# Two-layer hybrid encoder: order of the head products, value products and first weight splits

## The chip, the cores and the metric

The kernel runs on one core of one Trainium2 chip. The metric is the device time of one execution in microseconds (us), lower is better. Before the change it is 1668.3 us, the median of 3 runs (1664.87 to 1670.17). TensorE is called PE here, VectorE DVE, ScalarE ACT, GpSimd POOL and SyncE SP, as in the profile.

## The reference, cut to what matters

512 tokens, model width 1024, 8 heads, everything in float32.

```python
hn  = rms_norm(h, norm_mix[0]);  h += mlstm_mixer(hn, ...)               # layer 0
h  += swiglu(rms_norm(h, norm_ffn[0]), w_gate[0], w_up[0], w_down[0])
h  += sigmoid(rms_norm(h, norm_ple[0]) @ ple_gate[0]) * (p[0] @ ple_proj[0])
hn  = rms_norm(h, norm_mix[1])                                            # layer 1
proj = (hn @ b_w_in).reshape(B, S, 3, 3, 8, 128)       # group g, (q, k, v), head
# per group: rope(q), rope(k); window attention with dilation 1, 4, 16; merge by denominators
h  += o @ b_w_out[0]
h  += swiglu(rms_norm(h, norm_ffn[1]), ...);  h += (gated input);  out = rms_norm(h)
```

`rms_norm` is a factor per token, 1/sqrt(mean square + eps), times a weight per column. The factor per token can be multiplied in after a product, so a product with `hn` needs only the residual `h` times the column weight; the factor is needed when the product leaves PSUM.

## The kernel before, in words

**Residual and operands.** The residual is held transposed, as 8 tiles `hT[k]` of 128 columns x 512 tokens. `Norm.add(k)` (line 175) takes a finished `hT[k]`, multiplies by the column weights and splits the result into a rounded part `xh[k]` and a rest `xl[k]`, so that each product of two matrices is three matmuls (`mm3`, line 123: lines 124, 125, 126). `Norm.square(k)` adds the squares up in `q`; `Norm.stats` (line 244) makes the factor per token (`rcol`) with 8 small matmuls and five POOL operations; `Norm.bcast` (line 251) spreads it over all partitions as `rB`, either through two DMAs (lines 261 and 263) or, with `by_pe`, through 8 matmuls (line 255) and one DVE copy (line 258).

**Weights.** A weight tile of up to 1 MB comes by a DMA on SP's queue into one of 4 buffers (`wst`); `wsplit` (lines 116 and 117) splits it into `wh` on ACT and `wl` on DVE, 3 buffers each.

**PSUM.** There are 8 banks: 3 under the name `pj`, 3 under `s`, 2 under `o`. SBUF tiles of 2 KB per partition (`u`) share 58 buffers.

**Order.** The program is unrolled. Each engine's instructions are put in order when the program is built: earlier in the text goes first among those that the builder reckons to be ready at that moment. On the chip every engine then follows its fixed order.

**Layer 0's end and layer 1's start.** `ple(0)` (line 628) makes the 8 gate products and finishes `hT[0..7]` one by one: lines 658 (times `rB`), 659 (sigmoid), 660, 661 (add to `hT`), then `n1.add(k)`. `n1` also keeps sums of quarter blocks (`quad_sums`, lines 214 to 222, split in lines 207 and 208).

**Values.** `value_cell(g)` (line 773), three times, makes the values of group g for all heads with 7 instead of 8 block products (`product`, lines 784 to 797). Its weights are four quarters of 1 MB, added or subtracted in place on DVE (lines 807, 810). Its results are scaled by `rcol` (lines 803, 839) and stored to DRAM (lines 804, 840). In the first cell, between the fourth and the fifth product, come `n.stats()` and `n.bcast()` (lines 828, 829). After the third cell the tables `RS` and `RC` are multiplied by `rB` (lines 850 to 853).

**Heads.** `qk_head(h)` (line 887) makes q and k of three groups, 6 products of 24 matmuls, each evicted by `rope_evict` (line 855: DVE lines 858 and 860, POOL lines 861 and 863). `scores` (line 930) makes the probabilities, with two exchanges through DRAM (`swap`, line 739). `attend` (line 981) multiplies by the values. Before, the order is: three value cells, q and k of head 0, scores of head 0; then for each head h: values from DRAM (every second head), q and k of head h+1, `attend(h)`, scores of head h+1.

**Last head.** For the last head there are no next q and k; the loop computes the first 7 of 8 terms of three column blocks of `b_w_out` (`out_part`, line 1023) and finishes them after `attend`; the fourth block follows whole, then `colproj` (line 551) makes blocks 4 to 7. `residual` (line 566) adds each block to `hT` (line 568) and calls `nf.add`.

**Feed-forward.** `ffn` (line 580) begins with the first 256 columns of `w_gate` and `w_up`. It comes after `nf.stats()` and `nf.bcast()` in the text.

Of the kernel before, what the change touches and what calls it, by code (L numbers as in the profile page):

```python
# [15 lines left out]
ALU = mybir.AluOpType  # L16
# [20 lines left out]
def encoder_kernel(  # L37
# [513 lines left out]
    def colproj(src, xh, xl, nk, evict, ncols, first=0):  # L551

        for c2 in range(first, ncols // 256):
            o = [ps(), ps()]
            for k0 in range(0, nk, KT):
                kn = min(KT, nk - k0)
                st = wload(src, k0 * P, kn, 256 * c2)
                for cc in range(2):
                    wh, wl = wcols(st, kn, cc)
                    for k in range(kn):  # L560
                        mm3(o[cc], wh[:, k], wl[:, k], xh[k0 + k], xl[k0 + k],
                            k0 + k == 0, k0 + k == nk - 1)
                    if k0 + kn == nk:
                        evict(o[cc], 2 * c2 + cc)
# [6 lines left out]

    nf = Norm(NW_FFN)
    colproj(a_w_out[0], mh, ml, KT, residual(nf), D)
# [6 lines left out]
    def ffn(l, n, nxt):  # L580
        ah, al = [], []
        for j2 in range(JT // 2):
            sg = wload(w_gate[l], 0, KT, 256 * j2)
            su = wload(w_up[l], 0, KT, 256 * j2)
            for cc in range(2):
                og_ = ps()
                wh, wl = wcols(sg, KT, cc)
                for k in range(KT):
                    mm3(og_, wh[:, k], wl[:, k], n.xh[k], n.xl[k], k == 0, k == KT - 1)
                gt = ut()  # L590
                V.tensor_tensor(gt, og_, n.rB, op=ALU.mult)  # L591
                A.activation(gt, gt, AF.Silu)
                ou = ps("o", (P, S), 2)
                wh, wl = wcols(su, KT, cc)
                for k in range(KT):
                    mm3(ou, wh[:, k], wl[:, k], n.xh[k], n.xl[k], k == 0, k == KT - 1)
                u = ut()
                V.tensor_tensor(u, ou, n.rB, op=ALU.mult)  # L598
                V.tensor_tensor(u, u, gt, op=ALU.mult)
                hi, lo = ut(dt=F32R), ut(dt=F32R)  # L600
                A.copy(hi, u)
                V.tensor_tensor(lo, u, f(hi), op=ALU.subtract)
                ah.append(hi)
                al.append(lo)
        pt = ple_in(l)
        colproj(w_down[l], ah, al, JT, residual(nxt), D)
        return pt
# [142 lines left out]
    pt = ffn(0, nf, npl)  # L750
# [22 lines left out]
    def value_cell(g):  # L773
# [39 lines left out]
        m1, m5, u2, w_, c12, c22, c21, c11 = (two() for _ in range(8))  # L813
        b11, b12 = quarter(0, 0), quarter(0, 1)
        product(x_, "a11", b11)
        for t in range(2):
            A.copy(m1[t], x_[t])
        b22 = quarter(1, 1)
        product(z_, "s1", b11, plus(b12))
        for t in range(2):  # L820
            V.tensor_tensor(w_[t], z_[t], m1[t], op=ALU.subtract)
        product(y_, "s2", b11, plus(b22))
        for t in range(2):
# [3 lines left out]
        if g == 0:  # L827
            n.stats()
            n.bcast()
# [3 lines left out]
        product(y_, "s3", b12, plus(b22), first=False)  # L833
        for t in range(2):
            V.tensor_tensor(c22[t], y_[t], w_[t], op=ALU.add)
            store(t, 1, 1, c22[t])
        product(x_, "a12", b21, first=False)
        for t in range(2):
            A.activation(c11[t], x_[t], AF.Copy, scale=n.ra(t))
            nc.sync.dma_start(rows[t][:, 0:512], c11[t])  # L840
        product(y_, "a22", b11, neg_plus(b21), first=False)
        for t in range(2):
            V.tensor_tensor(c21[t], m1[t], y_[t], op=ALU.subtract)
            store(t, 1, 0, c21[t])

    for g in range(3):
        value_cell(g)

    rB = n.rB
    V.scalar_tensor_tensor(RS, RS, sgn, rB[0:32], op0=ALU.mult, op1=ALU.mult)  # L850
    V.tensor_tensor(RC[0:32], RC[0:32], rB[0:32], op=ALU.mult)
    A.copy(RC[32:64], rB[32:64])
    A.copy(RC[64:P], rB[64:P])
# [33 lines left out]
    def qk_head(h):  # L887

        res = {}
        for g in range(3):  # L890
            for s in range(2):
                c0 = col(g, s, h)
                stg = wp.tile([P, KT, 256], F32, tag="wst", name=nm("wst"), bufs=WST)
                nc.sync.dma_start(stg[:, :, :P], b_in[:, c0:c0 + P].rearrange("(k p) c -> p k c", p=P))
                wh, wl = wcols(stg, KT, 0)
                o = ps()
                for k in range(KT):
                    mm3(o, wh[:, k], wl[:, k], n.xh[k], n.xl[k], k == 0, k == KT - 1)
# [122 lines left out]
    out_w, out_o = [], []  # L1021

    def out_part(c, k0, k1):
        wh, wl = out_w[c]
        for k in range(k0, k1):
            mm3(out_o[c], wh[:, k], wl[:, k], mh[k], ml[k], k == 0, k == KT - 1)

    mh, ml = [], []
    probs = scores(qk_head(0))
    for h in range(NH):  # L1030
# [4 lines left out]
        else:  # L1035
            for c2 in range(2):
                st = wload(b_w_out[0], 0, KT, 256 * c2)
                for cc in range(2 - c2):
                    out_w.append(wcols(st, KT, cc))
                    out_o.append(ps())  # L1040
                    out_part(2 * c2 + cc, 0, KT - 1)
# [3 lines left out]
    for c in range(3):  # L1045
        out_part(c, KT - 1, KT)
        ev(out_o[c], c)
    out_w.append(wcols(st, KT, 1))
    out_o.append(ps())
    out_part(3, 0, KT)  # L1050
    ev(out_o[3], 3)
    colproj(b_w_out[0], mh, ml, KT, ev, D, 2)
# [5 lines left out]
    pt = ffn(1, nf, npl)  # L1058
# [125 lines left out]
```

## Time and profile before

| what | value |
|---|---|
| median of 3 runs | 1668.3 us |
| the profiled execution's own time | 1665.16 us |
| its span from first to last instruction | 1663.4 us |
| mean granted PE clock | 0.986 |
| busy: PE, DVE, ACT, POOL | 96%, 54%, 38%, 22% |

The profile is of one execution. Its lines are read as: engine, line of the kernel, operation, output<-input tile names without buffer numbers, and in brackets the engine's idle time before and what ended it. A stretch is given in us from the span's start. The granted clock is 1.00 at 2.4 GHz and 0.5 at 1.2 GHz. Matmul ends are modelled, so the distance between matmul starts says more than the duration of one.

### The profile page before, as it was taken

To read this page: it belongs to the slowest core of one execution; us is meant where nothing else is said; L and a number is where in the kernel's file an instruction comes from. 1 tells how busy PE (TensorE), PEld (TensorE's weight loads), DVE (VectorE), ACT (ScalarE), POOL (GpSimd) and SP (SyncE) were. 2 spreads that over 40 slices of the span, in tenths; PEclk is the share of its full clock that TensorE was granted. 3 is DMA by queue.
4 is the path that set the end of the run, shared out by engine and by line. 5 is a ranking of instruction groups with operands and counts; after the bars stand their busy time and mean duration, and the time that the engine had idled before them with its cause. 6 is when DMAs were issued, how large, how long until landed. Compare 5 with 4: busy or idle time off the path is not lost.

```text
span 1663.4 us, 20250 instructions
## 1 busy us (share of the span) xinstructions
PE 1602.9 (96%) x7868; PEld 1348.5 (81%) x7868; DVE 895.1 (54%) x1458; ACT 625.6 (38%) x1042; POOL 373.4 (22%) x455
## 2 busy tenths in 40 slices
PE   6999999999999999878999999999899999999998
PEld 5898988788888888656887888888787888888886
DVE  7655654644443334867856666666454444433353
ACT  5666543322322323544533333333233322323242
POOL 4455402000000100110046665656120000001100
PEclk9999999999999999988999999999999999999999
DMA  7322222432323213213454242425033232333221
GB/s 207 102 77 77 77 88 67 133 94 86 99 88 115 95 57 111 79 50 134 163 153 133 76 124 75 125 76 157 26 102 112 96 91 88 101 115 107 83 76 51
DMA packets 189761, 164.99 MB, mean 99 GB/s; under 512 B 17929, under 2 KB 173121, under 8 KB 189665
## 3 DMA queue, kind: packets, MB, share of 16 engines
q1 hardware_dynamic: 188528, 163.50, 31.9%
q8 instruction: 62, 1.02, 0.3%
q14 instruction: 35, 0.28, 0.1%
q10 hardware_dynamic: 1104, 0.13, 0.1%
q0 software_dynamic: 32, 0.07, 0.0%
HBM read 155.20 MB, written 8.48 MB: 98 GB/s over the span
## 4 chain that ended last, share of the span: by engine, by line
PE 85%; DVE 5%; DMA 3%; ACT 3%; POOL 2%; issue 1%; SPq 0%; POOLq 0%; ACTq 0%; DVEq 0%
PE pj L124 19%; PE pj L126 19%; PE pj L125 19%; PE o L126 4%; PE o L124 4%; PE o L125 4%; PE o L499 2%; PE o L1001 2%; DVE wl L117 1%; DMA rbd<-rs 1%; ACT wh L116 1%; PE o L795 1%; PE o L796 1%; PE pj L794 1%; PE pj L796 1%
## 5 line engine op out<-in xcount | busy, mean ns | idle before, releaser
L116 ACT CAST wh<-wst 128x1024 fp32r<-128x1024 f32 (+2 forms) x285 | 289.4, 1020 | 660.4 <-PE pj L125 400.7
L126 PE MATMUL pj<-u,wl 128*128 128x512 f32 x1352 | 527.4, 390 | 7.0 <-DVE wl L117 7.0
L125 PE MATMUL pj<-u,wh 128*128 128x512 f32 x1352 | 528.3, 391 | 1.4 <-DVE u L188 1.4
L124 PE MATMUL pj<-u,wh 128*128 128x512 f32 x1352 | 527.5, 390 | 0.9 <-ACT u L1013 0.7
L117 DVE TENSOR_TENSOR wl<-wst,wh 128x1024 fp32r<-128x1024 f32 (+2 forms) x281 | 337.5, 1202 | 199.8 <-ACT wh L116 199.2
L126 PEld LDWEIGHTS pj<-u,wl 128*128 128x128 f32 x1352 | 253.8, 188 | 61.7 <-DVE wl L117 9.8
L124 PEld LDWEIGHTS pj<-u,wh 128*128 128x128 f32 x1352 | 253.9, 188 | 54.0 <-ACT wh L116 1.3
L125 PEld LDWEIGHTS pj<-u,wh 128*128 128x128 f32 x1352 | 253.9, 188 | 53.3 <-DVE u L188 1.8
L242 POOL TENSOR_TENSOR u<-u,u 128x512 f32<-128x512 f32 x30 | 50.9, 1695 | 848.7 <-ACT u L238 848.4
L124 PE MATMUL o<-u,wh 128*128 128x512 f32 x352 | 136.9, 389 | 0.0
L125 PE MATMUL o<-u,wh 128*128 128x512 f32 x352 | 136.9, 389 | 0.0
L126 PE MATMUL o<-u,wl 128*128 128x512 f32 x352 | 136.9, 389 | 0.0
L861 POOL TENSOR_TENSOR u<-u,RS 32x512 f32<-32x512 f32 x48 | 85.0, 1771 | 212.9 <-DMA wst<-in_b_w_in_dram 106.8
L598 DVE TENSOR_TENSOR u<-o,u 128x512 f32<-128x512 f32 x44 | 30.4, 691 | 125.0 <-PE o L126 117.3
L863 POOL TENSOR_TENSOR u<-u,u 32x512 f32<-32x512 f32 x48 | 83.5, 1740 | 3.8
L124 PE MATMUL pj<-wh,u 128*128 128x256 f32 (+1 forms) x272 | 79.8, 295 | 3.3 <-DVE u L413 3.3
L591 DVE TENSOR_TENSOR u<-pj,u 128x512 f32<-128x512 f32 x44 | 30.4, 690 | 93.7 <-PE pj L126 79.7
L125 PE MATMUL pj<-wl,u 128*128 128x256 f32 (+1 forms) x272 | 79.9, 294 | 0.0
L126 PE MATMUL pj<-wh,u 128*128 128x256 f32 (+1 forms) x272 | 79.8, 294 | 0.0
L125 PEld LDWEIGHTS o<-u,wh 128*128 128x128 f32 x352 | 66.1, 188 | 13.9
L126 PEld LDWEIGHTS o<-u,wl 128*128 128x128 f32 x352 | 66.1, 188 | 13.7
L124 PEld LDWEIGHTS o<-u,wh 128*128 128x128 f32 x352 | 66.0, 187 | 13.6
(299 smaller groups left out, 2051.2 us busy)
## 6 DMA issues: line engine op xcount, KB each, us to landing
wst<-in_b_w_in_dram SPq DMA_DIRECT2D x48, 512.0 KB, 3.8
wst<-in_w_gate_dram SPq DMA_DIRECT2D x22, 1024.0 KB, 5.3
wst<-in_w_up_dram SPq DMA_DIRECT2D x22, 1024.0 KB, 5.3
wst<-in_w_down_dram SPq DMA_DIRECT2D x16, 1024.0 KB, 5.2
wst<-in_b_w_in_dram SPq DMA_DIRECT2D x12, 1024.0 KB, 6.2
wst<-in_a_w_in_dram SPq DMA_DIRECT2D x8, 1024.0 KB, 5.4
wst<-in_ple_gate_dram SPq DMA_DIRECT2D x8, 1024.0 KB, 5.1
wst<-in_w_down_dram SPq DMA_DIRECT2D x8, 768.0 KB, 4.6
```

The source lines that it names most:

```text
L116: A.copy(hi, src)
L117: eng.tensor_tensor(lo, src, f(hi), op=ALU.subtract)
L124: T.matmul(o, ah, bh, start=start, stop=False)
L125: T.matmul(o, ah, bl, start=False, stop=False)
L126: T.matmul(o, al, bh, start=False, stop=stop_)
L242: (G if k < KT - 1 else V).tensor_tensor(self.q, self.q, s, op=ALU.add)
L499: T.matmul(o[:, d, :], pt[d][s][:, j * P:(j + 1) * P], vt[s][:, hh, :], start=s == ks[0], stop=s == ks[-1])
L591: V.tensor_tensor(gt, og_, n.rB, op=ALU.mult)
L796: T.matmul(o[t], xl, wh[:, kk], start=False, stop=e == 1 and kk == 1, skip_group_check=True)
L861: G.tensor_tensor(sh, sh, RS, op=ALU.mult)
L863: G.tensor_tensor(d if b_layout else tok_a(d), d if b_layout else tok_a(d), to(sh), op=ALU.add)
L1001: T.matmul(a_tile(o, i) if bi < 2 else b_tile(o, i), vv[i][:, e * P:(e + 1) * P], pt[:, i * P:(i + 1) * P], start=bi == 0 and i == 0, stop ...
```

## The change

q and k of head 0 are computed ahead of the three value cells. Within `qk_head(0)` the first product comes first, then `n.stats()`, then the second product, then `n.bcast(by_pe=True)` and the scaling of `RS` and `RC`, then the evictions and the other four products. Within a value cell the result tiles are asked for where they are first written. In the last head four blocks of `b_w_out` are computed to 7 of 8 terms, the fourth in an `o` bank; the last term's weights are split into tiles of their own. `colproj` gets a hook called ahead of the last block's eviction; there the first `w_gate` tile is loaded and its first half split, in both layers.

```diff
-    def colproj(src, xh, xl, nk, evict, ncols, first=0):
+    def colproj(src, xh, xl, nk, evict, ncols, first=0, ahead=None):
...
                     if k0 + kn == nk:
+                        if ahead and c2 == ncols // 256 - 1 and cc:
+                            ahead()
                         evict(o[cc], 2 * c2 + cc)
...
+    def ffn_first(l):
+
+        sg = wload(w_gate[l], 0, KT, 0)
+        return sg, wcols(sg, KT, 0)
+
     nf = Norm(NW_FFN)
-    colproj(a_w_out[0], mh, ml, KT, residual(nf), D)
+    first = []
+    colproj(a_w_out[0], mh, ml, KT, residual(nf), D, ahead=lambda: first.append(ffn_first(0)))
...
-            sg = wload(w_gate[l], 0, KT, 256 * j2)
+            sg = wload(w_gate[l], 0, KT, 256 * j2) if j2 else first[0]
...
-                wh, wl = wcols(sg, KT, cc)
+                wh, wl = wcols(sg, KT, cc) if j2 + cc else first[1]
...
-        m1, m5, u2, w_, c12, c22, c21, c11 = (two() for _ in range(8))
...
+        m1 = two()
...
         product(z_, "s4", b22, first=False)
-        if g == 0:
-            n.stats()
-            n.bcast()
+        c12 = two()
...
-    for g in range(3):
-        value_cell(g)
-
-    rB = n.rB
-    V.scalar_tensor_tensor(RS, RS, sgn, rB[0:32], op0=ALU.mult, op1=ALU.mult)
-    V.tensor_tensor(RC[0:32], RC[0:32], rB[0:32], op=ALU.mult)
-    A.copy(RC[32:64], rB[32:64])
-    A.copy(RC[64:P], rB[64:P])
...
+        def product(g, s):
+            c0 = col(g, s, h)
+            stg = wp.tile([P, KT, 256], F32, tag="wst", name=nm("wst"), bufs=WST)
+            nc.sync.dma_start(stg[:, :, :P], b_in[:, c0:c0 + P].rearrange("(k p) c -> p k c", p=P))
+            wh, wl = wcols(stg, KT, 0)
+            o = ps()
+            for k in range(KT):
+                mm3(o, wh[:, k], wl[:, k], n.xh[k], n.xl[k], k == 0, k == KT - 1)
+            return o
+
+        ahead = {}
+        if h == 0:
+
+            ahead[0, 0] = product(0, 0)
+            n.stats()
+            ahead[0, 1] = product(0, 1)
+            n.bcast(by_pe=True)
+            rB = n.rB
+            V.scalar_tensor_tensor(RS, RS, sgn, rB[0:32], op0=ALU.mult, op1=ALU.mult)
+            V.tensor_tensor(RC[0:32], RC[0:32], rB[0:32], op=ALU.mult)
+            A.copy(RC[32:64], rB[32:64])
+            A.copy(RC[64:P], rB[64:P])
         for g in range(3):
             for s in range(2):
-                c0 = col(g, s, h)
...
+                o = ahead[g, s] if (g, s) in ahead else product(g, s)
...
-    out_w, out_o = [], []
-
-    def out_part(c, k0, k1):
-        wh, wl = out_w[c]
-        for k in range(k0, k1):
-            mm3(out_o[c], wh[:, k], wl[:, k], mh[k], ml[k], k == 0, k == KT - 1)
+    out_o, out_last = [], []
+
+    def out_ahead():
+        for c2 in range(2):
+            st = wload(b_w_out[0], 0, KT, 256 * c2)
+            hi, lo = ut((P, 256), F32R), ut((P, 256), F32R)
+            A.copy(hi, st[:, KT - 1])
+            V.tensor_tensor(lo, st[:, KT - 1], f(hi), op=ALU.subtract)
+            for cc in range(2):
+                out_last.append((hi[:, cc * P:(cc + 1) * P], lo[:, cc * P:(cc + 1) * P]))
+                wh, wl = wcols(st, KT - 1, cc)
+                o = ps() if len(out_o) < 3 else ps("o", (P, S), 2)
+                out_o.append(o)
+                for k in range(KT - 1):
+                    mm3(o, wh[:, k], wl[:, k], mh[k], ml[k], k == 0, False)
 
     mh, ml = [], []
-    probs = scores(qk_head(0))
+    qk = qk_head(0)
+    for g in range(3):
+        value_cell(g)
+    probs = scores(qk)
...
-            for c2 in range(2):
-                st = wload(b_w_out[0], 0, KT, 256 * c2)
-                for cc in range(2 - c2):
-                    out_w.append(wcols(st, KT, cc))
-                    out_o.append(ps())
-                    out_part(2 * c2 + cc, 0, KT - 1)
+            out_ahead()
...
-    for c in range(3):
-        out_part(c, KT - 1, KT)
+    first = []
+    for c in range(4):
+        mm3(out_o[c], *out_last[c], mh[KT - 1], ml[KT - 1], False, True)
         ev(out_o[c], c)
-    out_w.append(wcols(st, KT, 1))
-    out_o.append(ps())
-    out_part(3, 0, KT)
-    ev(out_o[3], 3)
-    colproj(b_w_out[0], mh, ml, KT, ev, D, 2)
+    colproj(b_w_out[0], mh, ml, KT, ev, D, 2, lambda: first.append(ffn_first(1)))
```

## Rows read from the trace of the kernel before

**Rows 1.** The page: busy us, share of the span, instructions of each engine.

```profile
PE 1602.9 (96%) x7868; PEld 1348.5 (81%) x7868; DVE 895.1 (54%) x1458; ACT 625.6 (38%) x1042; POOL 373.4 (22%) x455
```

**Rows 2.** Waits of PE, stretch 683 to 885: us in total, times, longest.

```profile
PE o L795 <- DVE wl L117: 10.5, 2, 7.4
PE pj L794 <- ACT u L207: 5.5, 1, 5.5
...
PE s L947 <- POOL u L863: 2.3, 1, 2.3
```

**Rows 3.** Windows of the value cells: busy us of each engine, granted clock.

```profile
core 0: us, PE busy (x) PEld busy (x) DVE busy (x) ACT busy (x) POOL busy (x), PEclk, DMA share, GB/s
...
694.50:768.10 73.60, 51.28 (x179) 39.24 (x179) 47.18 (x60) 31.90 (x42) 5.71 (x7) 0.79 0.23 79
768.10:806.10 38.00, 38.00 (x169) 31.40 (x168) 31.17 (x32) 20.45 (x24) 0.00 (x0) 1.00 0.51 171
806.10:844.10 38.00, 38.00 (x169) 31.45 (x169) 30.68 (x32) 20.91 (x24) 0.00 (x0) 1.00 0.38 120
844.10:876.80 32.70, 32.70 (x147) 27.09 (x146) 16.55 (x24) 9.57 (x16) 20.94 (x20) 1.00 0.46 136
```

**Rows 4.** Timeline of PE in the first cell: start, us, instruction, idle before.

```profile
715.98 0.63 PE L794 MATMUL o<-wh,u 128*128 128x512 f32 x1
716.40 0.63 PE L795 MATMUL o<-wl,u 128*128 128x512 f32 x1
```

**Rows 5.** Timeline of DVE around the last residual tiles of layer 0.

```profile
673.87 0.68 DVE L658 TENSOR_TENSOR u<-pj,u 128x512 f32<-128x512 f32 x1
...
678.81 0.69 DVE L183 TENSOR_TENSOR u<-u,u 128x512 fp32r<-128x512 f32 x1 [0.23 <-ACT u L182]
...
690.40 0.68 DVE L658 TENSOR_TENSOR u<-pj,u 128x512 f32<-128x512 f32 x1
...
695.43 1.21 DVE L807 TENSOR_TENSOR wst<-wst,wst 128x1024 f32<-128x1024 f32 x1
...
703.84 0.68 DVE L658 TENSOR_TENSOR u<-pj,u 128x512 f32<-128x512 f32 x1
...
716.63 0.68 DVE L658 TENSOR_TENSOR u<-pj,u 128x512 f32<-128x512 f32 x1
...
726.25 0.69 DVE L183 TENSOR_TENSOR u<-u,u 128x512 fp32r<-128x512 f32 x1 [0.22 <-ACT u L182]
```

**Rows 6.** The chain that ended last, in the first cell: start, us, what.

```profile
739.80 1.65 PE s L247 x8
...
744.80 9.04 DMA rbd<-rs
753.91 6.36 DMA u<-rbd
```

**Rows 7.** Timeline of layer 0's gated input: the broadcast by PE.

```profile
650.20 1.05 PE L255 MATMUL s<-ident,rs 128*128 128x128 f32 x8
...
652.39 0.68 DVE L258 COPY u<-s 128x512 f32<-128x512 f32 x1
```

**Rows 8.** Timeline of DVE: the first eviction of a q product.

```profile
849.64 1.11 DVE L858 TENSOR_TENSOR u<-pj,RC 128x512 f32<-128x512 f32 x1 [3.13 <-PE pj L126]
```

**Rows 9.** Windows of the heads' ends: a middle head's attend, then the last head.

```profile
1123.30:1129.20 5.90, 5.82 (x52) 5.50 (x50) 3.68 (x6) 2.12 (x3) 5.74 (x5) 1.00 0.32 89
...
1175.80:1189.40 13.60, 13.57 (x61) 10.91 (x59) 3.41 (x16) 4.26 (x17) 0.00 (x0) 1.00 0.03 1
1189.40:1193.20 3.80, 0.03 (x1) 0.06 (x2) 0.87 (x2) 0.00 (x0) 0.00 (x0) 1.00 0.07 1
1193.20:1200.70 7.50, 7.31 (x48) 6.79 (x48) 1.81 (x3) 1.21 (x3) 0.00 (x0) 0.77 0.01 2
```

**Rows 10.** Timelines of ACT and DVE at the end of layer 1's output product.

```profile
1226.88 1.05 ACT L116 CAST wh<-wst 128x1024 fp32r<-128x1024 f32 x1 [3.25 <-issue]
...
1232.50 0.69 DVE L568 TENSOR_TENSOR hT<-pj,hT 128x512 f32<-128x512 f32 x1 [2.65 <-PE pj L126]
```

More of the change, by code (lines that the diff above doesn't have):

```diff
@@ L577, in encoder_kernel, with ffn @@
     nf.bcast()
-    def ffn(l, n, nxt):
+    def ffn(l, n, nxt, first):
         ah, al = [], []
         for j2 in range(JT // 2):
-            sg = wload(w_gate[l], 0, KT, 256 * j2)
+            sg = wload(w_gate[l], 0, KT, 256 * j2) if j2 else first[0]
             su = wload(w_up[l], 0, KT, 256 * j2)
@@ L749, in encoder_kernel @@
     npl = Norm(NW_PLE)
-    pt = ffn(0, nf, npl)
+    pt = ffn(0, nf, npl, first[0])
     if stop == "ffn0":
@@ L819, in value_cell @@
         product(z_, "s1", b11, plus(b12))
+        w_ = two()
         for t in range(2):
@@ L822, in value_cell @@
         product(y_, "s2", b11, plus(b22))
+        u2 = two()
         for t in range(2):
@@ L833, in value_cell @@
         product(y_, "s3", b12, plus(b22), first=False)
+        c22 = two()
         for t in range(2):
@@ L837, in value_cell @@
         product(x_, "a12", b21, first=False)
+        c11 = two()
         for t in range(2):
@@ L841, in value_cell @@
         product(y_, "a22", b11, neg_plus(b21), first=False)
+        c21 = two()
         for t in range(2):
@@ L889, in qk_head @@
         res = {}
+        def product(g, s):
[18 more added lines that the diff above has]
+            A.copy(RC[64:P], rB[64:P])
         for g in range(3):
             for s in range(2):
-                c0 = col(g, s, h)
[L893 to L898, printed above, removed]
+                o = ahead[g, s] if (g, s) in ahead else product(g, s)
                 if g == 0 and s == 1:
@@ L1057, in encoder_kernel @@
     npl = Norm(NW_PLE + 8)
-    pt = ffn(1, nf, npl)
+    pt = ffn(1, nf, npl, first[0])
     if stop == "ffn1":
```

## The prediction

> **What bounds the kernel now.** I read the page first: PE is busy for 1602.9 of the span's 1663.4 us [rows 1], so the work of PE sets the time, and a change of order can win only where PE stands or runs slowly. The waits of PE say where. Around the value cells it stands 10.5 us for DVE's split, 5.5 us for ACT's split of a quarter sum, and 2.3 us for POOL ahead of the first scores [rows 2]. The windows give the size: the first value cell takes 73.6 us, the two others 38.0 us each with PE never idle [rows 3]. They do the same work, so the first one's excess is 35.6 us: 73.60 - 51.28 = 22.3 us idle, and the rest at a granted clock of 0.79 on average. The timeline shows what that is: matmuls start 0.42 us apart (716.40 - 715.98) [rows 4], where a cell's 168 matmuls in 38.0 us are 0.226 us apart, so this is the lower level, 1.2 GHz, after PE had stood. Why PE stands there is in DVE's queue: the sixth, seventh and eighth residual tiles of layer 0 are taken from PSUM (line 658) at 690.40, 703.84 and 716.63 only, with the cell's weight preparations of 1.21 us (line 807) between, and the last `xl` is done at 726.25 + 0.69 = 726.9 [rows 5]. Later in the cell the statistics' factor goes out and back through DRAM, 9.0 + 6.4 us [rows 6], and what needs `rB` holds ACT and DVE up; that is the longest wait, 7.4 us [rows 2].
>
> The other place is the last head: PE has 13.6 us of prepared work after the last scores, then 3.8 us of nothing, and `attend` takes 7.5 us at a clock of 0.77 where a middle head's takes 5.9 us [rows 9].
>
> **The change, part by part.** *q and k first.* The value cells no longer meet unfinished residual tiles. Cell 0 then should cost 38.0 us as the others do [rows 3]. Of the 35.6 us of excess, the 8 matmuls of the statistics (1.65 us [rows 6]) stay, so 33.9 us can go. The 2.3 us ahead of the first scores can go too, since cells now lie between the last rotation and the scores [rows 2]. Sum: 36.2 us removable.
>
> What comes in: the broadcast by PE, 8 matmuls of 1.05 us in all on PE and a copy of 0.68 us on DVE [rows 7]; two DMAs leave SP's queue. PE pays 1.05 us.
>
> What is late next: the heads' products need all eight residual tiles as well. PE ends layer 0's last gate product at 694.5. Each product has 21 of its 24 matmuls without the last tile, 21 x 0.226 = 4.7 us; the three `pj` banks allow three products. With all 72 matmuls (16.3 us), the statistics (1.65) and the broadcast (1.05) PE has 19.0 us of work, up to 713.5, before a bank must come free. A bank comes free after the first eviction, which needs the last tile, the square and its addition (2 x 0.65, estimated from the 0.6 to 0.7 us of DVE's operations of this size in [rows 5]), the statistics up to the factor (744.80 - 739.80 = 5.0 us [rows 6]), the broadcast 1.05 and copy 0.68 [rows 7], the tables' scaling (2 x 0.68, taken as two such copies) and the eviction (1.11 [rows 8] and a shuffle, estimated 0.7): 11.2 us after the last tile. When is that tile done? The tile's way from line 658 to the end of line 183 takes 5.6 us where the queue is clear (673.87 to 679.50) and 10.3 us where it is not (716.63 to 726.94) [rows 5]. Earliest: 694.5 + 5.6 = 700.1, bank at 711.3, no idle time. Latest: three tiles in series from 690.40 at 10.3 us, 721.3, bank at 732.5, 19 us idle. I take three in series at 5.6 us, since the cell's preparations now stand behind: 707.2, bank at 718.4, 4.9 us idle, and 2.5 us for about 11 matmuls at the lower clock behind it (0.2 us each). So 7.4 us of the gain are given back, with ends of 0 and 26 (19 idle, 7 of lower clock).
>
> A bubble of this kind repeats if SBUF's 58 buffers run short: ten tiles of head 0 now live through all three cells. Each product's eviction would then wait for a store, and PE for the eviction; the rows of the two later cells show no idle time with 16 result tiles asked for at once [rows 3], which the change spreads out, so I cost this at nothing (a rival below has its price). The Trainium skill, Perfetto Trace Analysis, section Identifying Performance Opportunities, says that a gap repeating on the engine that should be saturated can mean too little SBUF or PSUM for the next tile. By that rule alone, each of the three cells would have such gaps; the two clean cells speak against it so far.
>
> SP's queue: cell stores, values' loads and head 1's weights come close together now. Head 1's first weights take the buffers freed ahead of the last cell's end, as head 0's did, and that passage shows no wait: the 32.7 us after the last cell are fully busy [rows 3]. Price if not: one wait of some 9 us, as long as the way out through DRAM [rows 6].
>
> *Last head.* Four blocks of 21 matmuls instead of three: 84 x 0.226 = 19.0 us in place of 13.6, from 1175.8 to 1194.8; `attend` could start at 1193.2 [rows 9]. The 3.8 us are filled by work that stood behind, and with no pause ahead of it `attend` should take 5.9 in place of 7.5: 1.6 us. Against it: the fourth and fifth splits now fall into the exchange, and one of 1.05 us [rows 10] may stand ahead of the chain's small operations. I take 5.0 us of the 5.4, with ends of 2 and 6 (the short waits after `attend` may go too). The four small split operations per the last term lie beside busy PE in head 7.
>
> *First gate weights.* Their split is on ACT at 1226.88 already, before the last residual addition at 1232.50 [rows 10]; the text moves it ahead of something that it precedes. Zero, with ends of a loss or gain of 1.05 us per layer, one split.
>
> **Sum.** 36.2 - 1.05 - 7.4 + 5.0 + 0 = 32.8 us. The profiled execution took 1665.16 us, which gives 1632.4; the median of the runs is 3.1 us above it, so 1635.5. I give 1635.
>
> **The rivals.**
> 1. *The evictions stay late.* If layer 0's last tiles leave DVE no earlier in series than at the long price, 26 us come back: 32.8 - 18.6 = 14 us gain, 1654. For it: the tiles were 13 us apart [rows 5]. Against it: part of that was line 807's preparations, which are now later in the text. The PE order decides too: matmuls start in their fixed order, so a product's last term put ahead of the next product makes PE stand. 0.20.
> 2. *The change does not do what it says:* the builder's order puts the cells' work where it was, as it does with the gate split [rows 10], and only the last head pays: 1668.3 - 5 = 1663. Against it: the broadcast and tables are now needed by evictions that hold banks. 0.06.
> 3. *Slower: SBUF starves the cells.* Place: the result tiles of the three cells, with head 0's ten tiles alive. If each cell ran like the first one now, 73.6 us, the three would take 220.8 instead of 149.6: +71 us, less 2.3 and 5.0: 1732. It decides from 13 us per cell on, since 3 x 13 exceeds the 38 us of the other gains. Against it: the 38.0 us cells, and results that live shortly. 0.06.
>
> **How the numbers follow.** Forecast 0.68, rivals 0.20, 0.06, 0.06. The range goes from 1626, no idle time at the hand-over and 6 us in the last head (36.2 - 1.05 + 6 = 41, with a microsecond of the runs' scatter), to 1654, rival 1; the forecast's own is 1626 to 1645. A measurement of this kernel tells about 0.3% from no change, 5 us (the three runs lie 5.3 us apart). Rival 2 sits on that bound and is shared. Faster 0.91, the same 0.03, slower 0.06.
>
> **What would show it.** Right: three cells of 38 us each, at clock 1.00; the wait for line 207 and the long wait behind the DRAM broadcast gone; a wait of PE of some 5 us in the first three head products, for `xl` (line 183) or for an eviction (line 858); no idle time ahead of the last `attend`, which takes 5.9 us; the gate's first split where it was. Wrong: waits of PE above 10 us in head 0 (rival 1), evenly repeated gaps in the cells (rival 3), the cells still ahead on PE (rival 2), or time lost in heads 1 to 6, for which I have no mechanism.

## The result, and the profile after

The changed kernel takes 1648.3 us (median of 4 runs, 1647.31 to 1651.35), the kernel before 1667.95 us on the same chip (median of 4, 1664.87 to 1670.17): a ratio of 0.9887, 95% interval 0.9866 to 0.9907. It is faster by 19.6 us and lies inside the range, though only because the range was drawn out to rival 1's 1654 us: the forecast's own part of it ended at 1645. The forecast gain was 32.8 us. In the profiled pair the own times, 1647.69 us against 1665.16, differ by 17.5 us, and the spans are 1646.0 and 1663.4 us. So the question of this part is where some 15 us of the expected gain went.

The rows that answer to [rows 1], the page's first part:

```profile
PE 1597.0 (97%) x7876; PEld 1345.8 (82%) x7876; DVE 901.6 (55%) x1461; ACT 626.3 (38%) x1044; POOL 377.4 (23%) x455
```

The waits of PE from 690 to 890 us, to set beside [rows 2]; the value cell's matmuls are lines 802 to 804 now:

```profile
engine line waited for: us in total, times, longest us
PE pj L124 <- DVE u L862: 4.0, 1, 4.0
PE pj L124 <- ACT u L182: 2.8, 1, 2.8
PE s L255 <- POOL rs L281: 2.5, 1, 2.5
PE o L803 <- DVE wl L117: 1.4, 1, 1.4
PE pj L803 <- DVE wl L117: 1.2, 1, 1.2
PE s L247 <- DVE u L242: 1.1, 1, 1.1
```

The windows, to set beside [rows 3]: the passage from the end of layer 0's last gate product to the first value cell, then the three cells.

```profile
core 0: us, PE busy (x) PEld busy (x) DVE busy (x) ACT busy (x) POOL busy (x), PEclk, DMA share, GB/s
693.98:746.76 52.78, 42.39 (x164) 34.30 (x164) 35.94 (x54) 19.31 (x31) 20.94 (x24) 0.84 0.28 90
746.76:788.50 41.74, 39.02 (x170) 31.30 (x168) 35.34 (x32) 19.54 (x22) 12.81 (x6) 1.00 0.42 135
788.50:826.58 38.08, 38.08 (x170) 31.54 (x168) 31.65 (x34) 20.90 (x24) 0.00 (x0) 1.00 0.50 167
826.58:864.43 37.85, 37.85 (x168) 31.36 (x167) 30.54 (x33) 20.91 (x24) 0.61 (x2) 1.00 0.38 120
```

The first cell fell from 73.6 to 41.7 us, and the waits of 7.4 and 5.5 us of [rows 2] are gone. The second and third cell are as they were. But the passage ahead of the cells is dear: 52.8 us for work that the prediction's figures put at 35.3 us (144 matmuls of 0.226 us, 1.65 for the statistics, 1.05 for the broadcast). Of the excess of 17.5 us PE stands idle for 10.4 us, in the four waits of the list that are not in line 803; of the other 7.1 us the clock takes 5.7. Two windows, with the same columns, show it at the lower of its two levels, 1.2 GHz, each after PE had stood; PE is busy in them for 11.3 us, at half speed:

```profile
702.85:706.26 3.41, 3.15 (x7) 2.48 (x8) 3.10 (x5) 0.74 (x2) 1.52 (x1) 0.50 0.34 133
719.92:733.57 13.65, 8.16 (x22) 6.56 (x23) 6.23 (x11) 1.85 (x3) 4.13 (x9) 0.50 0.39 142
```

The timeline of DVE in that passage shows why, the counterpart of [rows 5]. Line 666 takes a tile from PSUM (the last three are shown), line 183 makes the last `xl`, line 242 adds its square, lines 220 to 222 and 208 are the quarter sums and their splits, line 117 the weight splits:

```profile
689.59 0.68 DVE L666 TENSOR_TENSOR u<-pj,u 128x512 f32<-128x512 f32 x1
...
697.66 0.68 DVE L666 TENSOR_TENSOR u<-pj,u 128x512 f32<-128x512 f32 x1
...
705.91 0.69 DVE L666 TENSOR_TENSOR u<-pj,u 128x512 f32<-128x512 f32 x1
...
710.77 0.69 DVE L183 TENSOR_TENSOR u<-u,u 128x512 fp32r<-128x512 f32 x1
711.38 0.42 DVE L222 TENSOR_TENSOR u<-u,u 128x256 f32<-128x256 f32 x1
711.71 1.29 DVE L208 TENSOR_TENSOR u<-u,u 128x512 fp32r<-128x512 f32 x2
713.29 1.23 DVE L117 TENSOR_TENSOR wl<-wst,wh 128x1024 fp32r<-128x1024 f32 x1 [0.29 <-ACT wh L116]
714.43 0.69 DVE L208 TENSOR_TENSOR u<-u,u 128x512 fp32r<-128x512 f32 x1
715.03 1.22 DVE L117 TENSOR_TENSOR wl<-wst,wh 128x1024 fp32r<-128x1024 f32 x1
716.16 0.69 DVE L242 TENSOR_TENSOR u<-u,u 128x512 f32<-128x512 f32 x1
...
723.51 0.69 DVE L258 COPY u<-s 128x512 f32<-128x512 f32 x1 [4.38 <-PE s L255]
...
726.63 0.71 DVE L862 STREAM_SHUFFLE u<-pj 32x512 f32<-32x512 f32 x1
```

The last tile is split at 711.46, not at 707.2 as I took, and the bank comes free at 727.34, which is 15.9 us after it and not 11.2. Between the tile and its square's addition stand a sum, three splits of sums and two weight splits: 716.85 - 711.46 = 5.4 us in place of the 1.3 that I had for it. The broadcast on PE lies in the second window of low clock and lasts 2.08 us in place of the 1.05 of [rows 7]:

```profile
721.40 2.08 PE L255 MATMUL s<-ident,rs 128*128 128x128 f32 x8 [2.46 <-POOL rs L281]
```

The last head answers to [rows 9]: prepared work from the last scores, idle time, `attend`.

```profile
1160.47:1180.64 20.17, 20.17 (x98) 16.67 (x96) 8.88 (x29) 7.34 (x21) 0.00 (x0) 1.00 0.37 106
1180.64:1182.65 2.01, 0.00 (x1) 0.03 (x1) 0.84 (x2) 0.90 (x1) 0.00 (x0) 1.00 0.87 266
1182.65:1190.20 7.55, 7.36 (x48) 6.93 (x48) 2.88 (x4) 1.22 (x3) 0.00 (x0) 0.77 0.20 69
```

From the start of the last scores PE has 20.2 us of work, where before it had 15.4 (1173.98 to 1189.4). Yet it still stands for 2.0 us, and `attend` still runs at a mean clock of 0.77: the probabilities come 22.2 us after the scores, where before they came after 19.2 (1193.17 - 1173.98).

### The profile page after: what moved, and what is told of

Read it like the earlier page. It is cut to its first block, busy times and chain, and to the rows that moved or that the text cites. A ratio compares the mean times of both kernels' runs of the same rounds, so it can differ in the third digit from the quotient of the medians.

```text
span 1646.0 us, 20291 instructions
## 1 busy us (share of the span) xinstructions
PE 1597.0 (97%) x7876; PEld 1345.8 (82%) x7876; DVE 901.6 (55%) x1461; ACT 626.3 (38%) x1044; POOL 377.4 (23%) x455
## 4 chain that ended last, share of the span: by engine, by line
PE 83%; DVE 6%; POOL 4%; ACT 3%; DMA 2%; issue 2%; SPq 0%; POOLq 0%; DVEq 0%; ACTq 0%
PE pj L124 18%; PE pj L126 18%; PE pj L125 18%; PE o L126 5%; PE o L124 5%; PE o L125 5%; PE o L499 2%; PE o L1020 2%; DVE wl L117 1%; POOL u L479 1%; PE s L966 1%; PE o L804 1%; PE o L802 1%; PE o L803 1%; PE pj L803 1%
## 5 line engine op out<-in xcount | busy, mean ns | idle before, releaser
L117 DVE TENSOR_TENSOR wl<-wst,wh 128x1024 fp32r<-128x1024 f32 (+3 forms) x281 | 336.1, 1197 | 194.7 <-ACT wh L116 194.2
L124 PE MATMUL o<-u,wh 128*128 128x512 f32 x359 | 139.7, 389 | 0.0
L125 PE MATMUL o<-u,wh 128*128 128x512 f32 x359 | 139.7, 389 | 0.0
```

Of the source, the lines that this page charges most:

```text
L117: eng.tensor_tensor(lo, src, f(hi), op=ALU.subtract)
L124: T.matmul(o, ah, bh, start=start, stop=False)
L125: T.matmul(o, ah, bl, start=False, stop=False)
```

## The experiments

All ratios are to the kernel before on the same chip. The kernels ran in four groups on four chips, and before measured 1660.9, 1661.1, 1667.3 and 1660.2 us there; so between groups I compare ratios. In-group differences in us are given for the first group, where the second run has the same order of instructions as the change and so serves as its control.

**The last head undone.** The loop for the last head as in the kernel before, all else as changed:

```diff
...
-            out_ahead()
+            for c2 in range(2):
+                st = wload(b_w_out[0], 0, KT, 256 * c2)
+                for cc in range(2 - c2):
+                    out_w.append(wcols(st, KT, cc))
+                    out_o.append(ps())
+                    out_part(2 * c2 + cc, 0, KT - 1)
...
```

> The last head as before (three blocks ahead, the fourth behind attend), all else as changed. My theory from the two traces: the change wins 3.4 us between the last scores and the feed-forward's statistics (62.1 us before, 58.7 us after), so this kernel takes 1648.3 + 3.4 = 1652 us, with the last attend starting 16.4 to 17.2 us after the last scores' second part is on PE and not 20.2 us. Rival: the earlier exchange ends by chance of the trace and the part is worth the 5.0 us of the forecast, 1653 us and more; or it is worth nothing, 1648 us.

It took 1647.74 us, ratio 0.992 (0.9906 to 0.9935), 3.46 us above the control. So the last head's part is worth some 3.5 us, as the theory ahead of this run had it, and not 5.0. With it undone the last head's scores are 18.7 us ahead of `attend`; with it, 21 to 22.

**The gate hook undone.**

```diff
-    colproj(a_w_out[0], mh, ml, KT, residual(nf), D, ahead=lambda: first.append(ffn_first(0)))
+    colproj(a_w_out[0], mh, ml, KT, residual(nf), D)
...
-    pt = ffn(0, nf, npl, first[0])
+    pt = ffn(0, nf, npl, ffn_first(0))
...
```

> The first gate weights loaded and split where they were before, all else as changed. Theory: zero, 1648 us within 1 us, and the same order on every engine. Rival: the hook pulls the split ahead and saves one split of 1.05 us in each layer, so this takes 1650 us.

1644.28 us, ratio 0.9896 (0.9881 to 0.9911), the same as the change within the intervals. Every engine's list of instructions is the same with and without the hook: the builder had put that split there already. In the trace of the changed kernel the gate's first split (line 116 on ACT) stands 11.1 us ahead of the last residual addition (line 570):

```profile
1204.56 1.06 ACT L116 CAST wh<-wst 128x1024 fp32r<-128x1024 f32 x1 [2.99 <-issue]
```

And the addition on DVE:

```profile
1215.62 0.69 DVE L570 TENSOR_TENSOR hT<-pj,hT 128x512 f32<-128x512 f32 x1 [2.65 <-PE pj L126]
```

In the kernel before it is the same distance: there the gate's first split is the one at 1221.44. The split of [rows 10], at 1226.88, is by the order of the weight splits the first one of `w_up`, so what [rows 10] is read for holds all the more.

**The sums later.** The quarter sums of tiles 4 to 7 are made after head 0's six products, no more within `add`:

```diff
-                self.quad_sums(k)
+                if k < 4:
+                    self.quad_sums(k)
...
     qk = qk_head(0)
+    for k in range(4, KT):
+        n.quad_sums(k)
```

> The quarter sums of tiles 4 to 7 (12 sums, 6 splits) are asked for behind q and k of head 0 and not within add(k). Theory A (DVE's and ACT's queues): these stand between the last residual tiles, and ahead of the last square; without them the last xl is done near 707 us in place of 711.5, and rB near 716 in place of 724; idle time at the hand-over falls from 13 to some 5 us and most of the 6 us lost at the lower clock goes: 1638 us. Theory B (the chain's own length): the tiles' way through PSUM, ACT and DVE binds, not what stands between; 1646 us or more.

1641.23 us, ratio 0.9877 (0.9862 to 0.9892): 3.05 us below the control, where about 10 was expected. The hand-over did clear: the tiles are taken 5.4 to 5.5 us apart, the last `xl` is done at 702.4 (701.69 + its 0.7), PE waits there 1.8 us in two pieces, and the cells begin at 731.2 instead of 745.3. But the first cell took 54.2 us instead of 42.3, with new waits for ACT's and DVE's splits, and the second cell began only 1.8 us earlier than in the control (the table below). The timeline of POOL in this run showed something I had not looked for (lines 864 and 866 are the rotation here):

```profile
728.48 5.21 POOL L864 TENSOR_TENSOR u<-u,RS 32x512 f32<-32x512 f32 x1
733.77 2.16 POOL L866 TENSOR_TENSOR u<-u,u 32x512 f32<-32x512 f32 x1
735.90 13.98 POOL L864 TENSOR_TENSOR u<-u,RS 32x512 f32<-32x512 f32 x1
749.96 1.26 POOL L866 TENSOR_TENSOR u<-u,u 32x512 f32<-32x512 f32 x1
```

The same operation takes 1.26 us at other places of this list and 13.98 us here, while DVE worked through its sums and splits without a pause. PE's longest wait in that cell, 5.9 us up to 756.21 for a split of ACT, leads back to it: ACT's copy ahead of that split stood until POOL's delayed row of operations had come to the addition that ends at 754.11.

```profile
754.14 1.07 ACT L826 COPY u<-pj 128x512 f32<-128x512 f32 x2 [8.18 <-POOL u L866]
```

**Two more banks.** The third and fourth product of head 0 go to the `o` banks, so PE needs no eviction before the sixth product:

```diff
-            o = ps()
+            o = ps("o", (P, S), 2) if h == 0 and g == 1 else ps()
```

> The two products of group 1 of head 0 go to the two o banks, so that PE has five products to work on ahead of rB. Theory C (PSUM binds): the stops of 1.1, 2.5 and 4.0 us ahead of and behind the statistics are filled by 48 more matmuls (10.9 us), and the lower clock behind them goes: 1636 us. Theory A: PE meets the statistics' matmuls in its fixed order before those products, so only the last stop of 4.0 us goes: 1643 us.

1639.6 us, ratio 0.9863 (0.9846 to 0.9879): 4.7 us below the control, near the smaller of the gains expected, but not by its reason: the stops of 1.1 and 2.5 us at the statistics and the broadcast did fall, to nothing and 0.5 us. PE's wait for a bank was not removed but moved, from the fourth product into the first cell (3.2 us, still for line 862), and of the 10.4 us by which the cells begin earlier the first one gives back 5.9: it takes 48.2 us.

**The sums spread** over head 0's evictions, two tiles after each of the k products of groups 0 and 1:

```diff
-                self.quad_sums(k)
+                if k < 4:
+                    self.quad_sums(k)
...
                 res[g, s] = t
+                if h == 0 and s == 1 and g < 2:
+                    n.quad_sums(4 + 2 * g)
+                    n.quad_sums(5 + 2 * g)
```

> As the run with the sums behind all of head 0's products, but the sums of tiles 4 and 5 are asked for behind group 0's eviction and those of 6 and 7 behind group 1's, so they come before the passage to the cells. Theory A2 (the sums' 9 us of DVE work only moved from one hand-over to the next, where POOL's rotations then stood for up to 14 us): no PE wait at the statistics, the cells start some 12 us earlier than with the change as it is, and the first cell takes some 40 us: 0.9896 - 0.006 = 0.984 of before. Rival (the sums cost PE time wherever they stand): 0.9877 as with the sums behind.

1640.15 us, ratio 0.9875 (0.9861 to 0.989): the rival's figure, and not the 0.984 expected. The statistics are early (703.7), but now PE waits 6.3 us for a bank, since sums and evictions share DVE. **Spread sums and the two banks together:**

> The same, with group 1's products in the two o banks. Theory: with the sums out of the way rB comes near 711 us, ahead of the time at which three banks run out (713.5), so the two more banks add nothing, 0.984 of before as e5. Rival (PSUM binds by itself): another 3 to 4 us as in e4, 0.982.

1641.96 us, ratio 0.9887 (0.9871 to 0.9902): no wait for a bank any more, cells begin at 731.6, and the first cell takes 54.7 us. Neither expected ratio, 0.984 or 0.982, came. Both attempts at the hand-over end where the others did.

**The rotation on DVE.** Only head 0's two POOL operations per product are moved to DVE (`eng` is DVE in head 0 and POOL in the other heads):

```diff
-        G.tensor_tensor(sh, sh, RS, op=ALU.mult)
+        eng.tensor_tensor(sh, sh, RS, op=ALU.mult)
...
```

> Head 0's six rotations on DVE and not on POOL, all else as changed. Theory P (DVE and POOL hold each other up where head 0's late rotations meet the first cell's weight preparations): a preparation takes 1.2 us and not 2.2, the first cell's waits of 1.2 and 1.45 us go, the first cell takes 38.2 and not 41.7 us: 0.9896 - 0.002 = 0.9875 of before. Rival (DVE's own order makes these waits, and has 12 more operations of 0.6 us now): same or up to 4 us slower, 0.990 to 0.992.

1639.0 us, ratio 0.9872 (0.9857 to 0.9888), as the theory had it. The waits ahead of the cells are the change's own, to the tenth (2.8, 1.1, 2.5, 4.0), and the first cell takes exactly what the second does:

```profile
744.34:782.42 38.08, 38.08 (x169) 31.54 (x168) 31.98 (x35) 19.55 (x22) 0.00 (x0) 1.00 0.46 149
```

DVE has more to do here (35 operations instead of 32 in the cell), and its busy time is less: 31.98 us against 35.34. In the changed kernel each preparation took longer while POOL rotated. The timelines of the two engines in the changed kernel, DVE first (line 815 is the preparation, 818 its subtracting form):

```profile
752.00 2.20 DVE L815 TENSOR_TENSOR wst<-wst,wst 128x1024 f32<-128x1024 f32 x1
754.13 2.32 DVE L117 TENSOR_TENSOR wl<-wst,wh 128x1024 fp32r<-128x1024 f32 x1
756.48 2.19 DVE L815 TENSOR_TENSOR wst<-wst,wst 128x1024 f32<-128x1024 f32 x1
758.60 2.31 DVE L117 TENSOR_TENSOR wl<-wst,wh 128x1024 fp32r<-128x1024 f32 x1
760.94 1.23 DVE L818 SCALAR_TENSOR_TENSOR wst<-wst,wst 128x1024 f32<-128x1024 f32 x1
```

And POOL in the same stretch:

```profile
750.72 2.40 POOL L863 TENSOR_TENSOR u<-u,RS 32x512 f32<-32x512 f32 x1
753.20 2.16 POOL L865 TENSOR_TENSOR u<-u,u 32x512 f32<-32x512 f32 x1
755.33 2.26 POOL L863 TENSOR_TENSOR u<-u,RS 32x512 f32<-32x512 f32 x1
757.66 2.15 POOL L865 TENSOR_TENSOR u<-u,u 32x512 f32<-32x512 f32 x1
```

The two engines take turns: an operation of 1.2 us on DVE and one of 1.26 on POOL each last 2.2 us and more, and when POOL's list ends at 759.8, DVE's next operation takes 1.23 us again.

**Last terms after `attend`.** The split of the eighth term is made after the head loop, on the theory that its two subtractions on DVE and the early load of `w_up` lengthen the last exchange:

```diff
-    def out_ahead():
-        for c2 in range(2):
-            st = wload(b_w_out[0], 0, KT, 256 * c2)
+    sts = []
+
+    def out_tail():
+        for st in sts:
             hi, lo = ut((P, 256), F32R), ut((P, 256), F32R)
...
     first = []
+    out_tail()
```

> In the last head the last terms' weights are split behind attend in the text, all else as changed. Theory L (the exchange ahead of the last attend is 3 us longer because the two small splits stand ahead of the maxima on DVE, 0.45 us, and because freeing the weight buffers early lets a 1 MB load of w_up run beside the exchange's DMAs, 1.8 us): the load moves behind the exchange, attend starts within 20.0 us of the last scores and not 22.2, PE's wait of 2.0 us and the lower clock behind it go: 3 us less, 0.988 of before. Rival (the fourth block's split between the chain's small DVE operations, 0.8 us, and chance in the DMAs): within 1 us of the change, 0.9896.

1643.2 us, ratio 0.9891 (0.9873 to 0.9909), no better. The maxima were ready 2.5 us after the scores instead of 3.0 and no load stood in the exchange, and still 21.5 us passed from scores to `attend`, within the 21.1 to 22.4 us of the runs whose last head is the change's. That theory fell. One piece of the lengthening remains in the trace of all kernels with this last head: a split (line 117) between two small operations of the chain, here in the changed kernel, at 1174.47.

```profile
1174.39 0.15 DVE L983 TENSOR_TENSOR e<-ng,mn 128x4 f32<-128x4 f32 x1
1174.47 1.22 DVE L117 TENSOR_TENSOR wl<-wst,wh 128x1024 fp32r<-128x1024 f32 x1
1175.60 0.15 DVE L986 TENSOR_TENSOR dn<-e,swo 128x4 f32<-128x4 f32 x1
```

**Both remedies: sums later, rotation on DVE.** The two edits above together:

> The quarter sums of tiles 4 to 7 come after the six products of head 0 (as in the third run), and head 0's rotation is on DVE in place of POOL (as in the seventh). Theory (two separate terms: DVE's queue sets the hand-over, and DVE and POOL hold each other up in cell 0): the hand-over keeps the waits of the third run (about 2 us in all, cells begin near 733), and cell 0 takes 38 to 42 us as in the seventh; together some 15 us less than the change, a ratio near 0.980 to the kernel before, about 1630. Rival (the sums are simply too much work for DVE between the last tile and cell 0, whoever rotates): cells begin near 733 and cell 0 takes 48 us or more, ratio 0.986 or above.

1643.44 us, ratio 0.9866 (0.9845 to 0.9888). My theory of two separate terms fell, the rival's numbers came: cells begin at 733.1, the first takes 49.7 us. POOL does nothing in that cell, and DVE is busy for 42.0 of the 49.7 us, 56 operations where a clean cell has 32 to 35:

```profile
733.06:782.78 49.72, 43.65 (x169) 33.89 (x168) 41.98 (x56) 23.16 (x28) 0.00 (x0) 0.90 0.34 107
```

**Spread sums, banks, rotation on DVE:**

> The sums of tiles 4 to 7 are spread over the products of head 0, the third and fourth product go to the two o banks, and head 0's rotation is on DVE. Without the last step the same kernel began its cells at 731.6 and took 54.7 us for cell 0. Theory (DVE and POOL hold each other up): cell 0 takes 38 to 44 us, ratio 0.978 to 0.983. Rival (DVE's amount of work): cell 0 stays above 48 us, ratio 0.985 or above.

1644.04 us, ratio 0.9862 (0.9846 to 0.9879); first cell 50.9 us (732.9 to 783.8). The rival's again.

**The last head's splits on POOL.** The two subtractions of the last term and the splits of the fourth and fifth block go to POOL, which has nothing to do there:

```diff
-            V.tensor_tensor(lo, st[:, KT - 1], f(hi), op=ALU.subtract)
+            G.tensor_tensor(lo, st[:, KT - 1], f(hi), op=ALU.subtract)
...
-                wh, wl = wcols(st, KT - 1, cc)
+                wh, wl = wcols(st, KT - 1, cc, G if len(out_o) == 3 else V)
...
-                    wh, wl = wcols(st, kn, cc)
+                    wh, wl = wcols(st, kn, cc, G if first and c2 == first and not cc else V)
```

> In the last head the two last-term subtractions and the splits of the fourth and fifth block run on POOL, which is idle there. Theory L2 (DVE's splits stand between the small operations of the exchange): the 0.45 us ahead of the maxima and the 0.8 us within the exchange go, scores to attend falls from 22.2 to about 20.9 us, and the time by 1.0 to 1.5 us, a ratio of about 0.9885 to the kernel before. Rival (the exchange through DRAM itself varies or is longer with loads beside it): scores to attend stays at 21.5 us or more and the time within 0.5 us. Second rival: POOL's splits are late (2 us and more each) and PE waits for the fourth block: 1 to 3 us slower than the change.

1652.6 us, ratio 0.9913 (0.9899 to 0.9928): above the change's 0.9887, but the intervals overlap, so that it is slower is not shown. It is no gain, and PE's list has no wait for the fourth block, which the second rival had named. The split is gone from the chain (0.43 us from line 983 to line 986 instead of 1.21), but the exchange itself grew, and scores to `attend` became 23.5 us. The timelines of SP and DVE show the place: a load of `w_up` is now issued ahead of the read of the first exchange (line 754), and the read arrives 1181.50 - 1175.72 = 5.8 us after its issue, where in the changed kernel, with that load behind it, it took 2.5 us (1171.62 to 1174.12).

```profile
1174.83 0.37 SPq L108 DMA_DIRECT2D wst<-in_w_up_dram  x1
1175.72 0.34 SPq L754 DMA_DIRECT2D swo<-swd  x1
```

DVE, the first four operations behind that read:

```profile
1181.50 0.16 DVE L981 TENSOR_TENSOR mn<-swo,ng 128x4 f32<-128x4 f32 x1 [13.62 <-DMA swo<-swd]
1181.70 0.16 DVE L982 TENSOR_TENSOR e<-swo,mn 128x4 f32<-128x4 f32 x1
1181.78 0.15 DVE L983 TENSOR_TENSOR e<-ng,mn 128x4 f32<-128x4 f32 x1
1182.21 0.16 DVE L986 TENSOR_TENSOR dn<-e,swo 128x4 f32<-128x4 f32 x1 [0.28 <-ACT e L984]
```

The longer way from scores to `attend`, 1.3 us against the change, would not make up the whole 0.0026 of ratio (some 4 us); in its profile layer 0, which the edit does not touch, ended 4.2 us later than in the change's, and that has no explanation here.

**The sums left out.** To take work away from DVE without moving any: the sums of tiles 4 to 7 are not computed, and the second, third and fourth product of each cell (the expectation below says fifth for fourth) read the sums of tiles 0 to 3 in their place. Six casts of 0.62 us on ACT go with them. PE's matmuls are all there.

```diff
...
-            V.tensor_tensor(s1, a[:, two], b[:, two], op=ALU.subtract)
-            V.tensor_tensor(s2, a[:, one], s1, op=ALU.subtract)
-            V.tensor_tensor(s4, b[:, one], s2, op=ALU.subtract)
             if j:
                 for e in ("s1", "s2", "s4"):
-                    split(e)
+                    self.sums.setdefault(e, []).append(self.sums["s3"][(k - 4) // 2])
```

> The quarter sums of tiles 4 to 7 are left out: 12 additions of 0.41 us and 6 subtractions of 0.67 us on DVE, 8.9 us of its work, and 6 casts on ACT; the second, third and fifth product of each value cell read the sums of tiles 0 to 3 in their place. Nothing else of the change is touched: head 0's rotation stays on POOL and every matmul stays. Theory (between the last residual tiles and the first cell's last product, the amount of work in DVE's queue sets the time): the whole 8.9 us come off the passage and a little more, since PE then keeps its clock: the square of the last tile follows it at once, cells begin near 732 as in the third run, and cell 0 takes 42 us or less, so that the second cell begins near 774 in place of 788; some 14 us less than the change, ratio 0.981. Rival (the rotation on POOL and DVE's work hold each other up, whatever the amount): cells begin near 732, cell 0 still takes 48 us or more, and the gain is 5 us or less, ratio 0.986 or above.

1632.33 us, ratio 0.9832 (0.9818 to 0.9845), between the theory's 0.981 and the rival's 0.986, and clear of both. The cells begin at 732.1 and the second at 776.6; counted from the end of layer 0 that is 11.5 us before the control's, for 8.9 us less of DVE's work (and 3.7 us less of ACT's). The first cell still takes 44.4 us: in it DVE is busy for 38.1 us with 34 operations, where the second cell's 34 fill 31.7 us in the changed kernel; beside them POOL rotates for 17.8 us.

```profile
732.14:776.58 44.44, 39.70 (x170) 31.16 (x168) 38.11 (x34) 19.51 (x22) 17.84 (x8) 1.00 0.39 128
```

Where the passage ends in each run, from the starts of the value cells' matmuls in the profiled executions. Some executions reach the end of layer 0 up to 5 us later than others, so the times are counted from there (the matmuls of line 247 for layer 0's gated input, at 643.95 us in the change):

| kernel | cells begin after | first cell | second begins after | ratio |
|---|---|---|---|---|
| the change | 102.8 | 41.7 | 144.6 | 0.9887 |
| its control (hook undone) | 102.2 | 42.3 | 144.5 | 0.9896 |
| sums later | 88.6 | 54.2 | 142.7 | 0.9877 |
| two more banks | 91.7 | 48.2 | 139.9 | 0.9863 |
| sums spread | 96.7 | 44.6 | 141.2 | 0.9875 |
| spread, banks | 88.5 | 54.7 | 143.2 | 0.9887 |
| rotation on DVE | 101.9 | 38.1 | 140.0 | 0.9872 |
| sums later, rotation on DVE | 88.6 | 49.7 | 138.3 | 0.9866 |
| spread, banks, rotation on DVE | 88.5 | 50.9 | 139.4 | 0.9862 |
| sums left out | 88.6 | 44.4 | 133.0 | 0.9832 |

Whatever clears the hand-over brings the cells' beginning forward by up to 14 us, and the first cell then gives back from two fifths to nine tenths of that, unless work leaves DVE. This fits a stretch, from layer 0's last tiles to the end of the first cell, that is set mostly by what DVE has to do in it, its collisions with POOL included: an order chose where PE waits, and gained at most some 6 us at the second cell here (with the rotation on DVE). Shown is only that leaving the sums out gains more than any order tried. DVE is not busy throughout: 71.3 of the 94.5 us from the last gate product to the second cell in the change, 63.2 of 83.0 without the sums. And no run takes the sums off DVE while it leaves their casts on ACT. No re-ordering that keeps the sums got below a ratio of 0.986, and among the four lowest (0.9862 to 0.9872) the intervals don't tell one from another. All four lie below the change's 0.9887; the two extra banks show it most directly, since their runs (1637.30 to 1642.75 us) lie wholly below the control's (1643.36 to 1645.57) on the same chip. Sums left out together with the rotation on DVE was not tried.

## Why the prediction was right, and where it was not

*Right.* The removed excess was there: the first cell's waits for the quarter sums and for what stood behind the broadcast through DRAM are gone, and the second and third cells take 38.08 and 37.85 us at clock 1.00 with results and head 0's tiles alive together, so SBUF does not starve them (rival 3). The work moved on the chip as the text says (against rival 2). The hook is worth nothing, as forecast. The sign came from reading the excess of one cell over its like. That the time lies inside the range owes something to its width: 1648.3 us is nearer to rival 1's 1654 than to the forecast's 1635, and of the prediction's own signs one against it came, waits of PE above 10 us in head 0 (10.4), while two for it did not, no idle time ahead of the last `attend` and 5.9 us for it (2.0 and 7.55 us). One reading was wrong without effect: 1226.88 in [rows 10] is not the gate's split.

*Wrong, step by step,* in the profiled pair, where 32.8 us were forecast and 17.5 measured:

| step of the prediction | forecast | measured | gain lost |
|---|---|---|---|
| "7.4 us of the gain are given back" at the hand-over | 7.4 | 17.5 | 10.1 |
| "Cell 0 then should cost 38.0 us" | 38.0 | 41.7 | 3.7 |
| the 2.3 us ahead of the first scores "can go too" | 2.3 | a wait of 1.45 in the next head's scores | 1.5 |
| the last head, "I take 5.0 us" | 5.0 | 4.0 in this pair (0.6 of it in head 6's `attend`), 3.5 between runs | 1.0 |

These add up to 16.3 us, against the 15.3 that are missing; half a microsecond of the difference is that the head's products began at 693.98 where the cells of before began at 694.50, and another 0.6 us came in after the last head (the change is 16.9 us ahead at layer 1's feed-forward statistics and 17.5 at the end).

*The hand-over* was the large one. Its mechanism was right, and rival 1 was nearer by its size than my forecast. The step that failed reads "I take three in series at 5.6 us, since the cell's preparations now stand behind". What stood there in their place I had not counted: `add` also makes quarter sums and their splits, and together with two weight splits they lie in DVE's queue between the tiles. They put 8.1 to 8.3 us between the takes of the last three tiles instead of 5.6, and 5.4 us instead of 1.3 between the last tile and its square's addition. That chain then released the bank 15.9 us after the tile; in the third run, where those sums stand later, the takes lie 5.4 to 5.5 us apart and the last tile is done 7.8 us sooner, counted from the end of layer 0. What the low clock takes, I had put at 2.5 us; it is 5.7.

*The first cell.* [rows 3] had the sign that I passed over: in the two clean cells POOL is busy for 0.00 us, so they were no measure for a cell beside which head 0's rotation runs. The seventh run, with the rotation on DVE, takes 38.08 us for it, so this was the whole of the 3.7 us.

*The two are tied.* What no step of mine had, and what my third, fifth and sixth expectations missed as well, is the amount of DVE's work in the passage. I had treated DVE's order as the fault; moved, the sums' 8.9 us only change place. Leaving them out, with their six casts on ACT, is worth 11.5 us at the second cell; moving them alone is worth 1.8 us there. That DVE's amount of work is what binds is argued from this, not shown by itself.

*The first scores.* The wait is no longer ahead of head 0's scores; one of 1.45 us, again for POOL's rotation, came up in head 1's, where before there was none. Only the difference was gained.

*The last head.* The filler did what it should: the 84 matmuls kept PE at work to 1180.64. But I priced the exchange as fixed, with one split of 1.05 us that "may stand ahead of the chain's small operations". It became 3.0 us longer: 0.45 us for the two subtractions ahead of the maxima, 0.8 us for a split within the chain, and the rest in the two passages through DRAM. In the eleventh run a load of 1 MB issued just ahead of the read goes with a long one: 5.8 us against 2.5. That the load is the cause is likely, but rests on this one trace; in the eighth run, with no load there, the read took 3.4 us, so what sets its length in the other kernels stays open.

## What to carry to other kernels

Before an idle stretch is booked as gain, add up what each other engine still has to do between the last input and the end of the stretch: if a helper queue has much to do there, a new order can move the wait without removing it. A clean copy of the same work elsewhere is a measure only if the other engines are doing the same beside it; look for columns that are zero in the clean windows. And when filler is moved under a latency chain, its operations on the chain's engine, and its loads on the chain's queue, belong in the price.

## What the runs showed of the hardware

DVE and POOL hold each other up. In the change an addition or a split on DVE with two SBUF inputs took 2.2 to 2.3 us in place of 1.2 while POOL's rotation ran, and POOL's 1.26 us operations took 2.1 to 2.4; DVE's operations with one input in PSUM did not slow: the eviction's multiplication (line 861 in the third run), at 734.70, took its usual 0.68 us beside POOL's addition of 733.77 to 735.93. In the third run one POOL operation of 1.26 us lasted 13.98 us under an unbroken row of DVE operations with two SBUF inputs. The Trainium skill, SBUF — State Buffer, section Who interferes with whom, states this as a rule: a DVE instruction with two SBUF inputs contends with a GpSimd instruction that reads SBUF, and the later one is blocked. The traces agree with it, and the 13.98 us show that the one blocked can miss many turns.

The other is the read of the exchange through DRAM in the last head: 1.7 us in the kernel before, 2.5 us in the changed kernel, 3.4 us in the eighth run, 5.8 us with a 1 MB load issued 0.9 us ahead of it in the eleventh, for the same 128x8 values.
